# S5 tables moved behind the SSD stage in wider operations, the convolution's tail queued one block later, and the first loads interleaved

## The chip, the cores and the metric

One core of one Trainium2 chip runs the program. Engines: TensorE (PE; its weight loads, PEld, overlap the products), VectorE (DVE), ScalarE (ACT), GpSimd (POOL) and SyncE (SP, which only issues transfers here). ACT, POOL and SP each have a queue of DMA issues that stand in order between the engine's other instructions. The metric is the device time of one execution in microseconds (us); less is better.

## The reference

A decoder step with two layers on 576 tokens: a prompt of 512 and eight sequences of 8 new tokens. Each layer's token mixer runs three branches on the same input and merges them with gates:

```python
gates, u, q, k, v, fg, z, xbc, dt_raw = split(h @ w_in[l])
y_s5, s5_re, s5_im = s5_branch(u, ...)
y_fox = fox_prompt(q, k, v, logf)
xbc_c = silu(causal_conv(xbc))
y_ssd, h_new = ssd_scan(...)
merged = gates0*(y_s5 @ w_s5) + gates1*(y_fox @ w_fox) + gates2*(y_ssd @ w_ssd)
out = merged @ w_o[l]
```

The S5 branch is a complex diagonal state space in 32 groups of 16 channels and 64 states: `x[t] = A x[t-1] + B u[t]`, `y = Re(C x) + D u`, with A and B made from `lam`, `log_dt` and `b` by a discretisation. The SSD branch takes a causal convolution of width 4 over 1024 channels, `silu`, and a scan in chunks of 128. After the mixer come a layer norm and a channel mixer: a dense SwiGLU in layer 0, eight experts in layer 1.

## The kernel before, in words

**Products.** An activation is kept as two tiles, `xh` and `xl` (a rounded part and its rest), and so is each weight block. `colblocks` (L297) goes over blocks of 128 columns of a weight: `wload` (L252) puts a load of 512 KB on SP's queue (three buffers `wr`), `wsplit` (L270) splits it in halves with a copy on ScalarE (`wh`, L98) and a subtraction on VectorE (`wl`, L107), and `mm3` (L285) makes 24 products a half-block of 288 tokens (L291 to L293) into one of two accumulators `mm`. A whole block is 48 products; "block" below means one of these.

**Head.** `load_x` (L235) loads five tiles of x (four of 128 prompt tokens, one of 64 sample tokens), transposes each in eight pieces on TensorE (L233) and splits the result. Then `u_proj` projects the S5 input `u` in half-blocks, four of the first 288 tokens and four of the rest. Hooks behind half-blocks call `load_params` (small parameter loads `prow` and `tokp`, a transposition, a few VectorE operations; `dexp`, L127, is an exponential by polynomial on VectorE, with tiles `ef` and `eki`) and `s5_prep(0)`.

**S5 tables.** `s5_prep` (L332) discretises, builds powers of A (`pw`, nine of them) and then, for four quarters of the groups, the tables `ca` (C times powers 0 to 8) and `bm` (B times powers 0 to 7). It goes power by power, with operations of 4 groups x 16 channels = 64 columns; `ca` on VectorE, `bm` on GpSimd in layer 0 and on VectorE in layer 1. The temporaries lie in `s5a`. `bm` is transposed to `bo`, a short convolution kernel is formed by products with `bbd` (L466) into `kz`, and the three tables go to DRAM (`CD`, `BD`, `KZ`) over GpSimd's queue. In layer 1 the tables are made inside the feed-forward stage before it.

**Convolution.** `conv` (L1001) projects the 1024 convolution channels, eight blocks. `ev_x` takes each accumulator out of PSUM: ScalarE copies it to `xp` (L98), and behind the second half the taps run for 512 prompt columns and 64 sample columns: one scaled copy on ScalarE into `cva` (L1024), three fused multiply-adds each on VectorE (L110); then a Tanh on ScalarE into `cvt` (L1027), one more VectorE operation, and a store to `XD` on ScalarE's queue (L1029). `xp`, `cva`, `cvt` share a ring of four buffers.

**The rest of the mixer.** `ssd` (chunks: masks `ma`, `mt`, loads `xc` of `XD`, products `yd`), `kqv_fox` (12 blocks of keys, queries and values, with prompt attention per head: `pf`, `pT`, `vt`, `kT`, `qT`), `s5_scan_and_out` (L479: state inputs from `UD` and `BD` as `bmu`, a scan on VectorE, then four groups of output products with `tu`, `cu` and `V`, L587 and L588, a Gelu, a store and a reload), `fox_sample` (pairs of sequences: paged keys `kpg` and values `vpg`, scores `pa` L949, outputs `po` L986), fillers (gate and z blocks), `s5_glu` (a gated linear unit on `y5h`) and `merge5`.

**Order.** The code is written stage by stage, but a scheduler sets each engine's order from the dependencies and a priority that follows the order in the code. So stages overlap: before the convolution ends the next stage's work stands between its products, and moving a call moves its instructions on every engine.

Of the kernel before, what the change touches and what calls it, by code (L numbers as in the profile page):

```python
# [19 lines left out]
P = 128  # L20
# [26 lines left out]
def decoder_step(ctx, tc, A, O):  # L47
# [187 lines left out]
    def load_x():  # L235
        xs = A["x_sample"].rearrange("b t d -> (b t) d")
        for i in range(5):
            n = P if i < 4 else 64
            src = A["x_prompt"][0, i * P:(i + 1) * P, :] if i < 4 else xs
            xt = U("A", [P, D], name="xt")  # L240
            sp.dma_start(out=xt[:n], in_=src)
            for k0 in (0, 4):
                pt = (PX, PF)[k0 // 4]("xp")
                pv = pt.rearrange("p (k t) -> p k t", k=4)
                for k in range(4):
                    tr(pv[:, k, :n], xt[:n, (k0 + k) * P:(k0 + k + 1) * P], n)
                s = slice(i * P, i * P + n)
                split(xh[:, k0:k0 + 4, s], xl[:, k0:k0 + 4, s], pv[:, :, :n])
# [83 lines left out]
    def s5_prep(l):  # L332
# [23 lines left out]
        t256 = s5a[:, 672:928].rearrange("p (g c) -> p g c", g=16)  # L356
# [79 lines left out]
        for q in range(4):  # L436
# [4 lines left out]
            t_, t2_ = t256[:, 0:4], t256[:, 4:8]  # L441
            cr, ci = cc[:, 0, gs], cc[:, 1, gs]
            for tau in range(9):
                pr_, pi_ = bc(pw[:, 0, tau, gs], 2, 16), bc(pw[:, 1, tau, gs], 2, 16)
                o0, o1 = ca[:, 0, :, tau, :], ca[:, 1, :, tau, :]
                mul(en, o0, cr, pr_)
                mul(en, t_, ci, pi_)
                sub(en, o0, o0, t_)
                mul(en, o1, cr, pi_)
                mul(en, t_, ci, pr_)  # L450
                stt(o1, o1, -1.0, t_, OP.mult, OP.subtract)
            for s in range(8):
                pr_, pi_ = bc(pw[:, 0, s, gs], 2, 16), bc(pw[:, 1, s, gs], 2, 16)
                cmul(dve if l else pool, bm[:, 0, :, s, :], bm[:, 1, :, s, :], pr_, pi_, bb[:, 0, gs], bb[:, 1, gs], t2_)
# [213 lines left out]
    def u_proj(l, hooks=()):  # L668
        us = {}

        def ev_u(j, h, o):
# [9 lines left out]
            for at, f in hooks:  # L681
                if (j, h) == at:
                    f(0)
# [1248 lines left out]
```

## Time and profile before

| what | value |
|---|---|
| median of 3 runs | 2440.81 us (2440.51 to 2442.37) |
| the profiled execution, its own time | 2439.51 us |
| its span in the profile | 2437.9 us |
| mean granted clock of TensorE | 0.966 |
| PE busy | 2282.9 us (94%) |
| PEld busy | 2158.8 us (89%) |
| DVE busy | 1621.9 us (67%) |
| ACT busy | 1144.4 us (47%) |
| POOL busy | 596.0 us (24%) |

The span runs from the first to the last instruction of the profiled execution; 1.6 us lie around it. "Busy" is the time in which an engine works, and its share of the span. The granted clock is 1 at full speed. A table of stretches gives busy time for pieces of the span; a wait is put down to what ended last before the waiting instruction started. The list by line groups like instructions; in it a line such as L101 or L107 can be that of a helper (`mul`, `sub`), so the tile names tell what it is.

### The profile page before, as it was taken

How to read it: one execution, taken by the hardware profiler on the slowest of the kernel's cores; microseconds unless marked ns; L12 is line 12 of the kernel's file. 1: busy time of each engine (PE TensorE's matmuls, PEld its weight loads, DVE VectorE, ACT ScalarE, POOL GpSimd, SP SyncE). 2: the span in 40 equal slices, each digit the busy share in tenths (PEclk: the TensorE clock that was granted, in tenths of full speed). 3: DMA queues.
4: the chain of work that ended last, by engine and by line, in shares of the span. 5: the costliest groups of instructions: out<-in, count | busy, mean ns of one | idle time of the engine just before them, and what ended most of it. 6: DMA issues, size and time to landing. Idle time of an engine off the chain costs nothing. (4 is left out here: it accounts for less than half of the span.)

```text
span 2437.9 us, 46161 instructions
## 1 busy us (share of the span) xinstructions
PE 2282.9 (94%) x17037; PEld 2158.8 (89%) x17038; DVE 1621.9 (67%) x4287; ACT 1144.4 (47%) x2553; POOL 596.0 (24%) x879
## 2 busy tenths in 40 slices
PE   8889998889999999999999999898999699999975
PEld 7889887679998999999899888788999599999974
DVE  7986695446478883334765975555447588888856
ACT  4435434425346323223654443353334477777753
POOL 5874233441020110000214332244003410000022
PEclk9999998889999999999999999999999799999997
DMA  8367558473345433223575575766333799999993
GB/s 203 108 209 202 171 158 203 120 228 94 93 134 133 117 121 105 81 87 94 135 207 166 152 184 156 169 182 204 88 92 113 209 267 255 255 256 253 254 256 86
DMA packets 591997, 402.32 MB, mean 165 GB/s; under 512 B 59254, under 2 KB 556199, under 8 KB 591731
## 3 DMA queue, kind: packets, MB, share of 16 engines
q1 hardware_dynamic: 480088, 240.75, 37.3%
q0 software_dynamic: 29008, 90.07, 13.4%
q10 hardware_dynamic: 82666, 68.46, 9.7%
q8 instruction: 136, 2.23, 0.4%
q14 instruction: 99, 0.80, 0.1%
HBM read 330.74 MB, written 68.57 MB: 164 GB/s over the span
## 5 line engine op out<-in xcount | busy, mean ns | idle before, releaser
L107 DVE TENSOR_TENSOR wl<-wr,wh 128x512 fp32r<-128x512 f32 x894 | 622.7, 707 | 382.4 <-ACT wh L98 359.3
L98 ACT ACTIVATE wh<-wr 128x512 fp32r<-128x512 f32 x894 | 552.6, 625 | 523.6 <-PE mm L292 366.7
L291 PE MATMUL mm<-xh,wh 128*128 128x288 f32 (+1 forms) x2048 | 618.9, 302 | 21.3 <-ACT xp L98 10.3
L292 PE MATMUL mm<-xl,wh 128*128 128x288 f32 (+1 forms) x2048 | 614.8, 300 | 0.0
L293 PE MATMUL mm<-xh,wl 128*128 128x288 f32 (+1 forms) x2048 | 612.1, 299 | 0.0
L291 PEld LDWEIGHTS mm<-xh,wh 128*128 128x128 f32 (+1 forms) x2048 | 387.4, 189 | 34.6 <-ACT xp L98 11.5
L292 PEld LDWEIGHTS mm<-xl,wh 128*128 128x128 f32 (+1 forms) x2048 | 387.5, 189 | 6.7 <-issue 4.4
L293 PEld LDWEIGHTS mm<-xh,wl 128*128 128x128 f32 (+1 forms) x2048 | 387.1, 189 | 3.6 <-issue 1.1
L1674 PE MATMUL mm<-xe,wh 128*128 128x352 f32 x448 | 132.1, 356 | 0.0
L1674 PE MATMUL pf<-xe,wh 128*128 128x352 f32 x448 | 130.5, 355 | 0.0
L1675 PE MATMUL pf<-xe,wl 128*128 128x176 f32 x512 | 117.3, 249 | 0.0
L1675 PE MATMUL mm<-xe,wl 128*128 128x176 f32 x512 | 117.1, 249 | 0.0
L291 PE MATMUL mm<-hq,wh 128*128 128x288 f32 x352 | 104.5, 297 | 0.2 <-DVE rf L104 0.2
L293 PE MATMUL mm<-hq,wl 128*128 128x288 f32 x352 | 104.2, 296 | 0.0
L292 PE MATMUL pf<-xl,wh 128*128 128x288 f32 x352 | 104.1, 296 | 0.0
L291 PE MATMUL pf<-xh,wh 128*128 128x288 f32 x352 | 103.9, 295 | 0.0
L293 PE MATMUL pf<-xh,wl 128*128 128x288 f32 x352 | 103.9, 295 | 0.0
L292 PE MATMUL mm<-hq,wh 128*128 128x288 f32 x352 | 103.7, 295 | 0.0
L1675 PEld LDWEIGHTS mm<-xe,wl 128*128 128x128 f32 x512 | 96.6, 192 | 0.0
L1675 PEld LDWEIGHTS pf<-xe,wl 128*128 128x128 f32 x512 | 96.6, 192 | 0.0
L110 DVE SCALAR_TENSOR_TENSOR gt<-gt,mm 128x288 f32<-128x288 f32 x96 | 43.3, 452 | 67.5 <-PE mm L293 52.9
L1674 PEld LDWEIGHTS mm<-xe,wh 128*128 128x128 f32 x448 | 85.4, 191 | 0.0
(665 smaller groups left out, 5448.2 us busy)
## 6 DMA issues: line engine op xcount, KB each, us to landing
wr<-in_w_in_dram SPq DMA_DIRECT2D x112, 512.0 KB
wr<-in_moe_w_gate_dram SPq DMA_DIRECT2D x64, 512.0 KB
wr<-in_moe_w_up_dram SPq DMA_DIRECT2D x64, 512.0 KB
wr<-in_moe_w_down_dram SPq DMA_DIRECT2D x64, 512.0 KB
wr<-in_w_o_dram SPq DMA_DIRECT2D x32, 512.0 KB
wr<-in_ffn_w_gate_dram SPq DMA_DIRECT2D x25, 512.0 KB
wr<-in_ffn_w_up_dram SPq DMA_DIRECT2D x25, 512.0 KB
wr<-in_ffn_w_down_dram SPq DMA_DIRECT2D x24, 448.0 KB
```

What stands on the lines that cost most here:

```text
L98: return act.activation(out, in_, AF.Copy)
L107: e.tensor_tensor(out, a, b, op=OP.subtract)
L110: dve.scalar_tensor_tensor(out, a, s, b, op0=op0, op1=op1)
L291: pe.matmul(o, lhsT=wh_[:, a, :m], rhs=x[0][:, k, s], start=(st and k == 0), stop=False)
L292: pe.matmul(o, lhsT=wh_[:, a, :m], rhs=x[1][:, k, s], start=False, stop=False)
L293: pe.matmul(o, lhsT=wl_[:, a, :m], rhs=x[0][:, k, s], start=False, stop=(sp_ and k == kt - 1))
L1674: pe.matmul(o, lhsT=h_[:, k % 4, :], rhs=xf, start=(k == 0), stop=False)
L1675: pe.matmul(o[:, 0:CAP], lhsT=l_[:, k % 4, :], rhs=x[:, k, 0], start=False, stop=False, skip_group_check=True)
```

## The change

Three parts of the mixer's start and one temporary:

- **Head.** `load_x` is cut into `x_dma` and `x_tr`. SP's queue gets three x tiles, the weights of the first two half-blocks (loaded ahead and handed to `colblocks` as `first`), then the other two x tiles; the transpositions of x tiles 3 and 4 become hooks behind the first and second half-block, the parameter loads a hook behind the third, the parameters' transposition one behind the first half-block of the second 288 tokens.
- **Convolution tail.** The Tanh, the last VectorE operation and the store of a block are kept as `pend` and issued with the next block, ordered behind the copy that empties its second accumulator. The result overwrites the input tile `xp`; `cvt` is gone. The two small GpSimd copies to `co` come first.
- **Tables.** `s5_prep(0)` is called behind `ssd(0)` in the code, not as a hook of the `u` projection. In both layers `ca` is made for all nine powers in one operation (576 columns) and `bm` for all eight (512 columns), six operations each per quarter. A new temporary `s5t` holds the intermediate products. `bm` stays on GpSimd in layer 0.

```diff
-    def load_x():
...
+    def x_dma(i):
...
+        sp.dma_start(out=xt[:n], in_=src)
+
+    def x_tr(i):
...
-    def colblocks(src, c0, ncol, kt, x, evac, by_half=False):
+    def colblocks(src, c0, ncol, kt, x, evac, by_half=False, first=()):
+        first = list(first)
...
-                w = wsplit(wload(src, c0 + j * P, P, kt), P, kt)
+                w = wsplit(first.pop(0) if first else wload(src, c0 + j * P, P, kt), P, kt)
...
+        s5t = U("R" if l else "A", [P, 1152], name="s5t")
...
-            t_, t2_ = t256[:, 0:4], t256[:, 4:8]
-            cr, ci = cc[:, 0, gs], cc[:, 1, gs]
-            for tau in range(9):
-                pr_, pi_ = bc(pw[:, 0, tau, gs], 2, 16), bc(pw[:, 1, tau, gs], 2, 16)
-                o0, o1 = ca[:, 0, :, tau, :], ca[:, 1, :, tau, :]
-                mul(en, o0, cr, pr_)
...
-            for s in range(8):
...
-                cmul(dve if l else pool, bm[:, 0, :, s, :], bm[:, 1, :, s, :], pr_, pi_, bb[:, 0, gs], bb[:, 1, gs], t2_)
+            t_ = s5t[:, 0:576].rearrange("p (g t c) -> p g t c", g=4, t=9)
+            t2_ = s5t[:, 576:1088].rearrange("p (g t c) -> p g t c", g=4, t=8)
+            cr, ci = bc(cc[:, 0, gs], 2, 9), bc(cc[:, 1, gs], 2, 9)
+            pr_, pi_ = [bc(pw[:, i, :, gs].rearrange("p t g -> p g t"), 3, 16) for i in range(2)]
+            o0, o1 = ca[:, 0], ca[:, 1]
+            mul(en, o0, cr, pr_)
+            mul(en, t_, ci, pi_)
+            sub(en, o0, o0, t_)
+            mul(en, o1, cr, pi_)
+            mul(en, t_, ci, pr_)
+            stt(o1, o1, -1.0, t_, OP.mult, OP.subtract)
+            cmul(dve if l else pool, bm[:, 0], bm[:, 1], pr_[:, :, 0:8], pi_[:, :, 0:8],
+                 bc(bb[:, 0, gs], 2, 8), bc(bb[:, 1, gs], 2, 8), t2_)
...
         conv(l, w_in)
         ssd(l)
+        if l == 0:
+            s5_prep(0)
         kqv_fox(l, w_in)
...
+        def tail(j, x, a_, after):
+            t_ = x[:, 0:T]
+            with tc.issue_after(after.ins) if after is not None else nullcontext():
+                act.activation(t_, a_, AF.Tanh)
+                stt(t_, t_, 1.0, a_, OP.add, OP.mult)
+                act.dma_start(out=XD[l][j], in_=t_)
+        pend = []
...
+            i_ = cp(xs_[:, :, 3:11], o[:, 224:288].rearrange("p (b t) -> p b t", b=8))
...
+            if pend:
+                tail(*pend.pop(), i_)
...
-            act.activation(t_, a_, AF.Tanh)
-            stt(t_, t_, 1.0, a_, OP.add, OP.mult)
-            act.dma_start(out=XD[l][j], in_=t_)
...
+            pend.append((j, x, a_))
         colblocks(w_in, C_XBC, 1024, 8, X, ev_x)
+        tail(*pend.pop(), None)
...
-        load_x()
-        u_proj(0, (((1,0), load_params), ((0,1), s5_prep)))
+        for i in range(3):
+            x_dma(i)
+        uw = [wload(A["w_in"][0], C_U + j * P, P, 8) for j in range(2)]
+        for i in (3, 4):
+            x_dma(i)
+        for i in range(3):
+            x_tr(i)
+        u_proj(0, (((0, 0), lambda: x_tr(3)), ((1, 0), lambda: x_tr(4)), ((2, 0), lambda: params_dma(0)),
+                   ((0, 1), lambda: params_tr(0))), uw)
         mixer(0)
```

In the rows of order below, a row is one instruction (or several alike, x4) with its line, the tile it writes, the tiles it reads and the shape. A load of `wr` is a weight block's.

SyncE's queue at the head, before and then now:

```order
L221 DMA lb<-in_page_table_dram 128x16
L241 DMA xt<-in_x_prompt_dram 128x1024 x4
L241 DMA xt<-in_x_sample_dram 64x1024
L262 DMA wr<-in_w_in_dram 128x8x128 x2
L653 DMA prow<-in_b_gate_dram 24x128
```

```order
L221 DMA lb<-in_page_table_dram 128x16
L241 DMA xt<-in_x_prompt_dram 128x1024 x3
L266 DMA wr<-in_w_in_dram 128x8x128 x2
L241 DMA xt<-in_x_prompt_dram 128x1024
L241 DMA xt<-in_x_sample_dram 64x1024
L266 DMA wr<-in_w_in_dram 128x8x128
L664 DMA prow<-in_b_gate_dram 24x128
```

Two weight loads moved ahead of the last x tiles, and the parameter loads (`prow` and on, 13 in all) behind a third. The 14 table loads, which stood behind six `wr` loads, now stand behind all eight of the `u` projection and the eight of the convolution.

VectorE in the stretch around one convolution block, before and then now (`ssp` belongs to the forget gate's logarithm):

```order
L101 TENSOR_TENSOR s5a<-s5b,s5a 128x64
L101 TENSOR_TENSOR ssp<-ssp 128x80
L107 TENSOR_TENSOR wl<-wr,wh 128x512
L110 SCALAR_TENSOR_TENSOR cva<-xp,prm_184,cva 128x512
L110 SCALAR_TENSOR_TENSOR cva<-xp,prm_184,cva 128x64
L107 TENSOR_TENSOR ca<-ca,s5a 128x4x16
L720 TENSOR_SCALAR ssp<-ssp 128x80
L107 TENSOR_TENSOR wl<-wr,wh 128x512
L110 SCALAR_TENSOR_TENSOR kz<-id_78,dq,p_776 128x16
L1009 MEMSET xp 128x3
L1013 COPY xp<-cs_1421 128x8x3
```

```order
L110 SCALAR_TENSOR_TENSOR xp<-xp,cva 128x576
L734 TENSOR_SCALAR ssp<-ssp 128x80
L110 SCALAR_TENSOR_TENSOR cva<-xp,prm_184,cva 128x512
L1033 MEMSET xp 128x3
L1037 COPY xp<-cs_728 128x8x3
L101 TENSOR_TENSOR ssp<-ssp 128x80
L110 SCALAR_TENSOR_TENSOR cva<-xp,prm_184,cva 128x64
L110 SCALAR_TENSOR_TENSOR cva<-xp,prm_184,cva 128x512
L734 TENSOR_SCALAR ssp<-ssp 128x80
L110 SCALAR_TENSOR_TENSOR cva<-xp,prm_184,cva 128x64
L110 SCALAR_TENSOR_TENSOR cva<-xp,prm_184,cva 128x512
```

The 64-column operations on `s5a`, `ca` and the `kz` are gone from between the block's taps, and the operation that finishes a block (`xp<-xp,cva`, before on `cvt`) stands among the next block's.

TensorE where the first S5 output product with the state (`V`) comes; `mm` rows are a filler block's last products. Before and then now:

```order
L291 MATMUL mm<-xh,wh 128x288
L292 MATMUL mm<-xl,wh 128x288
L293 MATMUL mm<-xh,wl 128x288
L861 MATMUL pf<-pT,vt 64x128 x2
L588 MATMUL p_4679<-V_4344,cu 128x72
L587 MATMUL p_4679<-uc_4326,tu 128x72
```

```order
L297 MATMUL mm<-xh,wl 128x288
L233 MATMUL px<-ident,kpg 128x128
L877 MATMUL pf<-pT,vt 64x128 x2
L233 MATMUL pf<-ident,s 128x128 x3
L854 MATMUL pf<-kT,qT 128x384 x2
L965 MATMUL pa<-kk,lq 32x256 x2
L877 MATMUL pf<-pT,vt 64x128 x3
L854 MATMUL pf<-kT,qT 128x512 x2
L877 MATMUL pf<-pT,vt 64x128 x4
L593 MATMUL p_4312<-V_3977,cu 128x72
L592 MATMUL p_4312<-uc_3959,tu 128x72
```

The output products moved behind attention scores (`kT,qT`), sample scores (`kk,lq`) and page transpositions (`kpg`), and behind the last of the filler blocks: before, one of the 36 blocks ahead of the S5 output stood behind the first of them. Earlier in TensorE's order, the last product with `bbd` stands behind 21 blocks before and 24 now. The first product of the gated unit (`y5h`) stood behind the first of the four sample pairs (`po`) before and stands behind the second now.

## Rows read from the trace of the kernel before

**Rows 1.** stretches: us; PE, PEld, DVE, ACT, POOL busy (instructions); clock, DMA, GB/s

```profile
60.00:160.00 100.00, 82.88 (x601) 79.25 (x600) 99.11 (x324) 43.57 (x96) 88.22 (x198) 0.94 0.49 149
160.00:300.00 140.00, 139.98 (x1105) 129.44 (x1105) 91.68 (x228) 65.45 (x165) 52.55 (x82) 0.98 0.69 192
850.00:900.00 50.00, 50.00 (x402) 49.28 (x402) 42.74 (x203) 14.95 (x27) 8.56 (x10) 1.00 0.43 130
```

**Rows 2.** waits of TensorE, 60 to 160 us: engine, line, releaser: us, times, longest

```profile
PE mm L291 <- ACT xp L98: 9.4, 4, 3.8
PE yd L1109 <- DVE mt L101: 5.3, 1, 5.3
```

**Rows 3.** VectorE's groups, 0 to 300 us: count, busy us, mean ns, idle before

```profile
L101 DVE TENSOR_TENSOR s5a<-s5b,s5a 128x64 f32<-128x64 f32 x72 | 21.3, 296 | 0.8
L101 DVE TENSOR_TENSOR ca<-s5b,s5a 128x64 f32<-128x64 f32 x72 | 19.0, 326 | 0.0
L107 DVE TENSOR_TENSOR ca<-ca,s5a 128x64 f32<-128x64 f32 x36 | 12.3, 342 | 0.5
L110 DVE SCALAR_TENSOR_TENSOR ca<-ca,s5a 128x64 f32<-128x64 f32 x36 | 10.1, 280 | 0.4
L101 DVE TENSOR_TENSOR ma<-tri,ads 128x512 fp32r<-128x512 f32 x8 | 7.9, 990 | 0.0
L101 DVE TENSOR_TENSOR mt<-mt,bt 128x512 f32<-128x512 f32 x8 | 5.5, 702 | 0.2
```

**Rows 4.** GpSimd's groups, 0 to 300 us, the same columns

```profile
L101 POOL TENSOR_TENSOR s5a<-s5a,s5b 128x64 f32<-128x64 f32 x64 | 26.3, 410 | 3.8
L104 POOL TENSOR_TENSOR bm<-bm,s5a 128x64 f32<-128x64 f32 x32 | 19.7, 616 | 2.1
L101 POOL TENSOR_TENSOR bm<-s5a,s5b 128x64 f32<-128x64 f32 x64 | 18.2, 319 | 0.1
L101 POOL TENSOR_TENSOR ma<-tri,ads 128x512 fp32r<-128x512 f32 x8 | 9.4, 1179 | 0.0
```

**Rows 5.** TensorE in order of time, head: start, us, work [idle before <- releaser]

```profile
5.89 5.35 PE L233 MATMUL xp<-ident,xt 128*128 128x128 f32 x24 [5.89 <-DMA xt<-in_x_prompt_dram]
15.69 0.61 PE L291 MATMUL mm<-xh,wh 128*128 128x288 f32 x1 [1.64 <-ACT wh L98]
19.41 0.41 PE L233 MATMUL px<-ident,prow 104*128 104x104 f32 x1 [2.88 <-DMA tokp<-in_b_fgate_dram]
```

**Rows 6.** accumulators emptied, layers 0 and 1: min/median/max ns, first to last start

```profile
L98 ACT ACTIVATE xp<-mm x24: 218/348/415, 59.3 to 129.6; 128x288 f32<-128x288 f32 x8, 128x224 f32<-128x224 f32 x8, 128x64 f32<-128x64 f32 x8
L98 ACT ACTIVATE xp<-mm x24: 219/340/412, 1241.6 to 1295.1; 128x288 f32<-128x288 f32 x8, 128x224 f32<-128x224 f32 x8, 128x64 f32<-128x64 f32 x8
```

**Rows 7.** who waited for the convolution's VectorE chain, layer 0: us, times

```profile
  ACT cvt L1027: 14.6, 6
```

**Rows 8.** the S5 chain's places in order of time, TensorE and ScalarE's queue

```profile
211.82 0.67 PE L466 MATMUL p<-ca,bbd 128*32 128x128 f32 x16
241.48 0.27 PE L233 MATMUL p<-ident,sh 128*128 128x128 f32 x1
242.08 0.33 ACTq L497 DMA_DIRECT2D bmu<-BD  x1
386.12 0.44 PE L588 MATMUL p<-V,cu 128*128 128x72 f32 x2
406.01 0.41 PE L838 MATMUL pf<-kT,qT 128*128 128x128 f32 x2 [2.40 <-DMA qT<-QD]
451.00 0.85 PE L291 MATMUL mm<-y5h,wh 128*128 128x288 f32 x2 [0.16 <-ACT y5h L117]
460.81 1.07 PE L949 MATMUL pa<-kk,lq 128*32 128x256 f32 x4
467.50 0.62 PE L986 MATMUL po<-vpg,pTs 128*32 128x128 f32 x16
```

**Rows 9.** a table product of layer 1 on VectorE, 560 to 960 us

```profile
L101 DVE TENSOR_TENSOR s5a<-s5b,s5a 128x64 f32<-128x64 f32 x72 | 16.0, 222 | 0.1
```

More of the change, by code (lines that the diff above doesn't have):

```diff
@@ L233, in tr @@
         pe.transpose(out, in_, ident[:n, :n])
-    def load_x():
[L236 to L248, printed above, removed]
+    xts = {}
+    def x_dma(i):
+        n = P if i < 4 else 64
+        src = A["x_prompt"][0, i * P:(i + 1) * P, :] if i < 4 else A["x_sample"].rearrange("b t d -> (b t) d")
+        xts[i] = xt = U("A", [P, D], name="xt")
+        sp.dma_start(out=xt[:n], in_=src)
+    def x_tr(i):
+        n = P if i < 4 else 64
+        xt = xts[i]
+        for k0 in (0, 4):
+            pt = (PX, PF)[k0 // 4]("xp")
+            pv = pt.rearrange("p (k t) -> p k t", k=4)
+            for k in range(4):
+                tr(pv[:, k, :n], xt[:n, (k0 + k) * P:(k0 + k + 1) * P], n)
+            s = slice(i * P, i * P + n)
+            split(xh[:, k0:k0 + 4, s], xl[:, k0:k0 + 4, s], pv[:, :, :n])
     WB = dict(pool=wp, wr=3, wh=4, wl=4, body=False)
@@ L353, in s5_prep @@
         s5b = UA([P, 1152], name="s5b")
+        s5t = U("R" if l else "A", [P, 1152], name="s5t")
         sm = s5a[:, 0:384].rearrange("p (a g) -> p a g", g=16)
         pw = s5a[:, 384:672].rearrange("p (i t g) -> p i t g", i=2, t=9)
-        t256 = s5a[:, 672:928].rearrange("p (g c) -> p g c", g=16)
+        t256 = s5t[:, 0:256].rearrange("p (g c) -> p g c", g=16)
         bb = s5b[:, 0:512].rearrange("p (i g c) -> p i g c", i=2, g=16)
@@ L643, in decoder_step, with params_dma @@
     R_BG, R_L1G, R_L1B, R_L2G, R_L2B, R_CW, R_CB, R_GLU, R_NW = 0, 24, 32, 40, 48, 56, 88, 96, 100
+    prow = {}
     def load_params(l):
-        rows = V5("prow")[:104, 0:P]
+        params_dma(l)
+        params_tr(l)
+    def params_dma(l):
+        prow[l] = rows = V5("prow")[:104, 0:P]
         for nm, r0, n in (("b_gate", R_BG, 24), ("ln1_g", R_L1G, 8), ("ln1_b", R_L1B, 8), ("ln2_g", R_L2G, 8),
@@ L653, in load_params, with params_tr @@
             sp.dma_start(out=rows[r0:r0 + n], in_=s.rearrange("(r c) -> r c", c=P))
+        for i, nm in enumerate(("b_fgate", "ssd_dt_bias", "ssd_a_log", "ssd_d")):
+            sp.dma_start(out=tokp[l][:, i * 8:(i + 1) * 8], in_=A[nm][l].unsqueeze(0).to_broadcast([P, 8]))
+    def params_tr(l):
+        rows = prow[l]
         pt = PX()
@@ L660, in load_params @@
         dve.tensor_scalar(bglu[l], prm[l][:, R_GLU:R_GLU + 4], 0.5, None, op0=OP.mult)
-        for i, nm in enumerate(("b_fgate", "ssd_dt_bias", "ssd_a_log", "ssd_d")):
-            sp.dma_start(out=tokp[l][:, i * 8:(i + 1) * 8], in_=A[nm][l].unsqueeze(0).to_broadcast([P, 8]))
         dexp(tokp[l][:, 16:24], tokp[l][:, 16:24], 8)
@@ L666, in decoder_step, with u_proj @@
     S = dict(nc=nc)
-    def u_proj(l, hooks=()):
+    def u_proj(l, hooks=(), first=()):
         us = {}
@@ L682, in ev_u @@
                 if (j, h) == at:
-                    f(0)
-        colblocks(A["w_in"][l], C_U, 512, 8, X, ev_u, by_half=True)
+                    f()
+        colblocks(A["w_in"][l], C_U, 512, 8, X, ev_u, by_half=True, first=first)
     def mixer(l):
@@ L1016, in ev_x @@
             cp(x[:, 291:515], o[:, 0:224])
-            cp(xs_[:, :, 3:11], o[:, 224:288].rearrange("p (b t) -> p b t", b=8))
+            i_ = cp(xs_[:, :, 3:11], o[:, 224:288].rearrange("p (b t) -> p b t", b=8))
+            pool.tensor_copy(co[:, j, 0:3], x[:, 512:515])
+            pool.tensor_copy(co[:, j, 3:27].rearrange("p (b t) -> p b t", b=8), xs_[:, :, 8:11])
+            if pend:
+                tail(*pend.pop(), i_)
             wc = lambda q: pr[:, R_CW + q * 8 + j:R_CW + q * 8 + j + 1]
@@ L1020, in ev_x @@
             a_ = wk.tile([P, T], F32, name="cva", tag="xp", bufs=4)
-            t_ = wk.tile([P, T], F32, name="cvt", tag="xp", bufs=4)
             for dst, src in ((a_[:, 0:512], lambda q: x[:, q:q + 512]),
```

8 lines of the change are left out of this document (removed).

## Prediction

> **What bounds the kernel now.** I read the summary of busy time first (the table above): TensorE works 94% of the span, so only stretches in which it waits, or works at the lower clock, can give time back. The table of stretches shows such a place near the start [rows 1]: from 60 to 160 us TensorE is busy 82.88 of 100 us and its granted clock is 0.94, while VectorE is busy 99.11 of 100 and GpSimd 88.22. From 160 to 300 us the picture is turned round: TensorE 139.98 of 140, VectorE 91.68. The waits name what TensorE lacked [rows 2]: 9.4 us for ScalarE to empty a convolution block's accumulator (four waits) and 5.3 us for a VectorE product of the SSD stage. That is 14.7 of the 17.1 us missing between 60 and 160. The list by line and shape says what fills VectorE there [rows 3]: 216 operations of 64 columns on `ca`, 21.3 + 19.0 + 12.3 + 10.1 = 62.7 us; and GpSimd [rows 4]: 160 of 192 on `bm`, 26.3 + 19.7 + 18.2 = 64.2 us (32 subtractions come to these). These are the first layer's S5 tables. **VectorE, loaded with tables, paces the convolution.** After it TensorE is the bound, with VectorE a third idle.
>
> **The change part by part.**
>
> *Head.* Before, the first product starts at 15.69 us [rows 5], behind five loads of x, and the second group waits another 2.88 us for the parameters' transposition, which stands second in TensorE's order. The first x tile is used at 5.89; between there and 15.69 some 1.75 MB of x and 0.5 MB of weights arrive in 9.8 us, 0.23 MB/us. In the new order 0.75 MB (x tile 4 and the samples) stand behind the first weights: 0.75/0.23 = 3.3 us earlier. The 2.88 us go too. Against that, the 16 held-back transpositions now fall between products, the second half-block's first product stands in the first one's sequence and waits for the second weights, and VectorE's `ef` reads the parameter load before it splits the third half-block. I take 3.5 us; the ends are 0 and 6.2.
>
> *Convolution.* What do eight blocks cost without tables beside them? The same loop runs in layer 1, where no tables are made. From the first to the last emptying of an accumulator there are 129.6 - 59.3 = 70.3 us in layer 0 and 1295.1 - 1241.6 = 53.5 us in layer 1 [rows 6]: **17 us**. The queued tail belongs to this term: ScalarE now waits 14.6 us in six places for VectorE's chain before its Tanh [rows 7], with the next block's weight split and emptying queued behind. Behind the next block's emptying that wait is covered by the block's 48 products, 6.0 us at 402 TensorE instructions in 50 us [rows 1]. Its own price without the tables is about nothing: layer 1 has the Tanh wait too and keeps the pace of its products. Using the input tile for the result frees one of the ring's four slots; I count nothing for it. Some small VectorE work of the discretisation stays in the stage, so 17 is taken with ends 10 and 17.
>
> *SSD stage.* The wait of 5.3 us [rows 2] comes from a VectorE that is still behind; the 2.4 us that these two waits leave of the 17.1 I take for shorter ones of the same kind. Of both together 7.5 us go; if the moved tables hold VectorE there, nothing goes.
>
> *Tables.* They don't vanish: 24 operations of 576 columns replace 216. The nearest row without GpSimd beside it is 702 ns for 512 columns, the nearest with it 990 ns [rows 3]: 0.79 or 1.11 us each, 19 or 27 us in place of 62.7. On GpSimd 24 operations of 512 columns at 1.179 us [rows 4] make 28 us in place of more than 64. They land in the stretch that has 48 us of VectorE to spare [rows 1] and which loses the old tables' second half, so they cost nothing on the path; without that cover it would be up to 27 us. TensorE's part (16 products in 0.67 us [rows 8] and eight transpositions a group) only changes place: the two groups that ran inside the convolution come back later, 3 us by that row.
>
> That the chip's port weighs long GpSimd operations differently is a rule to set against this. The row: a 64-column product takes 296 ns beside GpSimd's tables [rows 3] and 222 ns in layer 1 without them [rows 9], so it is stretched by a third, not held for the 410 ns of a GpSimd product [rows 4]. The Trainium skill ("SBUF — State Buffer", section "SBUF: two separate sides") says the shared port pair is an exclusive lock, and that the loser blocks for the whole instruction; by that rule longer GpSimd operations would hold VectorE longer, and the trace agrees only in part. By the row the sum below stands; by the rule it would come out as rival 3 does.
>
> *Queues.* The tables' 14 loads leave SP's place ahead of the convolution's weights and now stand ahead of the attention weights, covered by three weight buffers. Their 12 stores move on GpSimd's queue to a place among the loads of `xc`, keys and queries, and those loads stand there behind the long operations too: six a group, 6 x 1.179 us [rows 4] = 7 us at most for one load. I count nothing, since TensorE has projections to do beside the attention, and 7 us as the upper end.
>
> *Layer 1.* Its tables are made in the feed-forward stage, where such products were 72 of 222 ns [rows 9] and become 8: less work for VectorE, but TensorE is busy 50.00 of 50 beside it [rows 1]. Nothing.
>
> Up to the 24th of the 36 weight blocks that are done before the S5 output this makes -3.5 - 17 - 7.5 + 3 = **-25 us**.
>
> **What of it reaches the end.** The S5 branch is a chain: tables, state inputs, scan, four output groups, store and reload, gated linear unit, merge. Its last table product stands behind block 21 before and block 24 now. Before, block 24 passes at 241.48 us [rows 8]; less 25 that is 216.5, against 211.82. So the chain starts 5 us later than it did, while all else is 25 us early. It has slack: the tables were in memory soon after 212, yet the first group's state inputs were asked for only at 242.08 [rows 8], by ScalarE's order. In the new order the first S5 output product with the state stands behind all filler blocks, which end at about 406.01; less 25 that is 381, against 386.12: 5 us gained there. From there to the gated unit's start at 451.00 [rows 8] were 64.9 us for four groups with attention heads between; one head and a half stood there, now half a head, so I take 4 us off. Behind the gated unit's start stood one pair of the sample attention (from 460.81 to 467.50, 7 us), which the new order has ahead of it. 5 + 4 + 7 = 16, if the chain decides; 25 if TensorE's work does. I take **18**: nearer the chain, since it has the tighter rows.
>
> The profiled execution took 2439.5 us; less 18 that is 2421.5. The median of the runs is 1.3 above it, so I forecast **2422.5**, with 2412 to 2431 as its own range.
>
> **Rivals.** (1) *All of it arrives and more.* If the output groups, freed of the filler, follow each other without pause, the 25 and the 7 add: 2440.8 - 32 = 2409. For it: TensorE waits in the stretch behind 406, as for the 2.40 us there [rows 8]. Chance 0.12. (2) *The chain keeps its length.* Table to gated unit took 451.0 - 211.8 = 239 us; starting 5 us later and saving only the 7 behind it, the end moves by 2: 2439. Against it: the slack to 242.08. Chance 0.10. (3) *GpSimd's long operations hold VectorE.* If each of 24 blocks VectorE for its 1.179 us, 28 us are added to 27 of tables in a stretch with 48 to spare; VectorE would again pace TensorE and a loss like that of the old stage, 17 us, comes back: 2440. Against it the third by which rows are stretched. Chance 0.05. (4) *Slower: the S5 chain decides and the convolution gains little.* If ScalarE or the loads hold the convolution back so that only 10 us are gained up to block 24, the last table product comes at 231.5, 20 us late; with the chain's old length, less 7, the end is 13 us late: 2454. It decides from a table product later than 219 (211.8 + 7). Against it: layer 1's pace. Chance 0.07.
>
> **Numbers.** Forecast 0.66, rivals 0.12, 0.10, 0.05, 0.07. A difference under 0.2%, 4.9 us, can't be told from none. Faster: forecast, rival 1, and the edge of rivals 2 and 3, 0.80; same 0.13; slower 0.07. The range from 2404 to 2439 leaves out rival 4 and the far end of rival 1.
>
> **What would show it.** Right: the spacing of the first and last accumulator emptying in layer 0 falls from 70 to some 55 us; the 60 to 160 stretch has TensorE near 98 of 100 at clock 1.0; `ca` has 24 rows of 0.8 to 1.1 us; the first product is at 12 to 13 us; the gated unit starts at 435 to 445. Wrong: VectorE still above 95% in the convolution; a wait of TensorE on an S5 product after block 25; the gated unit at or behind 451; or a stall of the attention weights behind the table loads.

## The result: slower by 0.74%

| | median | range | runs |
|---|---|---|---|
| before | 2440.35 us | 2436.07 to 2446.29 | 8 |
| changed | 2456.69 us | 2449.07 to 2468.85 | 8 |

The ratio is 1.0074, with a 95% interval of 1.0056 to 1.0092. On another chip, timed again beside the kernel before, it was 1.0093 (1.0060 to 1.0126). The forecast was a gain of 0.75%, with a chance of 0.07 for slower; the time lies outside its range.

The profiled execution of the changed kernel is its longest run, 2468.85 us (span 2467.2), 12 us over the median. In it the first products and the emptied accumulators of the convolution answer to [rows 5] and [rows 6]; TensorE's timeline first, then the accumulators of layer 0 and layer 1:

```profile
12.34 0.40 PE L295 MATMUL mm<-xh,wh 128*128 128x288 f32 x1 [1.26 <-ACT wh L98]
```

```profile
L98 ACT ACTIVATE xp<-mm x24: 220/340/415, 55.0 to 105.4; 128x288 f32<-128x288 f32 x8, 128x224 f32<-128x224 f32 x8, 128x64 f32<-128x64 f32 x8
L98 ACT ACTIVATE xp<-mm x24: 220/340/414, 1260.8 to 1312.6; 128x288 f32<-128x288 f32 x8, 128x224 f32<-128x224 f32 x8, 128x64 f32<-128x64 f32 x8
```

So the head is 3.35 us earlier and the convolution takes 50.4 us from first to last emptying, where it took 70.3. What came behind it is seen in the table of stretches, its columns as in [rows 1]:

```profile
60.00:160.00 100.00, 88.50 (x649) 86.73 (x649) 84.27 (x252) 49.27 (x105) 40.37 (x60) 0.93 0.52 150
160.00:300.00 140.00, 126.87 (x979) 113.72 (x978) 103.86 (x174) 58.73 (x153) 63.61 (x72) 0.96 0.65 192
850.00:900.00 50.00, 50.00 (x412) 48.91 (x411) 31.24 (x57) 16.24 (x32) 7.01 (x11) 1.00 0.43 139
```

TensorE now lacks 13.1 us in a stretch (160 to 300 us) in which it had lacked 0.02, and VectorE is busy 103.86 us there in place of 91.68, with fewer instructions (174 in place of 228). TensorE's waits from 60 to 300 us, columns as in [rows 2]:

```profile
PE yd L1133 <- DVE mt L101: 14.2, 2, 10.0
PE p L233 <- DVE smx L861: 3.0, 1, 3.0
PE pf L854 <- DVE s L110: 2.4, 1, 2.4
```

The accumulators' waits (9.4 us) are gone; the SSD products' wait for VectorE's `mt` has grown from 5.3 to 14.2 us. The longest, 9.97 us, ends at 140.05 us, and what follows it runs at half the clock for 6.5 us (the table of stretches again):

```profile
130.00:140.00 10.00, 0.07 (x1) 0.00 (x0) 10.00 (x16) 0.69 (x2) 6.78 (x8) 0.65 0.45 148
140.00:146.50 6.50, 6.45 (x28) 6.45 (x29) 2.90 (x14) 0.60 (x1) 0.00 (x0) 0.50 0.60 189
146.50:152.00 5.50, 5.50 (x43) 5.50 (x42) 1.36 (x3) 2.35 (x5) 2.26 (x3) 0.99 0.29 86
```

The operations that took the place of those in [rows 3] and [rows 4], VectorE and then GpSimd, 0 to 300 us:

```profile
L101 DVE TENSOR_TENSOR ca<-s5b,s5a 128x576 f32<-128x576 f32 x8 | 8.8, 1135 | 0.0
L107 DVE TENSOR_TENSOR ca<-ca,s5t 128x576 f32<-128x576 f32 x4 | 8.3, 2077 | 0.0
L101 DVE TENSOR_TENSOR s5t<-s5b,s5a 128x576 f32<-128x576 f32 x8 | 8.0, 1001 | 0.0
L799 DVE COPY qS<-kq 128x64 f32<-128x64 f32 x4 | 3.6, 891 | 2.8 <-ACT kq L798 2.8
L110 DVE SCALAR_TENSOR_TENSOR ca<-ca,s5t 128x576 f32<-128x576 f32 x4 | 3.4, 839 | 0.0
L101 DVE TENSOR_TENSOR ptmp<-s5a 128x32 f32<-128x32 f32 x2 | 2.7, 1346 | 0.0
```

```profile
L101 POOL TENSOR_TENSOR bm<-s5a,s5b 128x512 f32<-128x512 f32 x8 | 10.4, 1312 | 3.2 <-PE p L233 3.1
L101 POOL TENSOR_TENSOR s5t<-s5a,s5b 128x512 f32<-128x512 f32 x8 | 9.4, 1179 | 0.2
L104 POOL TENSOR_TENSOR bm<-bm,s5t 128x512 f32<-128x512 f32 x4 | 5.6, 1400 | 0.0
L107 POOL TENSOR_TENSOR bm<-bm,s5t 128x512 f32<-128x512 f32 x4 | 5.5, 1378 | 0.0
```

The tables' own time is near the prediction's upper estimate: 28.5 us on VectorE (27 there) and 30.9 on GpSimd (28). But these means hide two kinds of operation. Of the two products of 32 columns (mean 1346 ns) one took 0.18 us and one 2.51; of the four `ca` subtractions (mean 2077 ns) two took 0.74, one 1.60 and one 5.22. Time order shows what the long ones stood for. VectorE, then GpSimd (start, us, work):

```profile
127.65 1.14 DVE L419 COPY a<-s5a 128x32 f32<-128x32 f32 x1
...
130.96 1.28 DVE L101 TENSOR_TENSOR a<-a 128x16 f32<-128x16 f32 x1
132.16 0.16 DVE L101 TENSOR_TENSOR ptmp<-a 128x16 f32<-128x16 f32 x1
132.25 0.16 DVE L101 TENSOR_TENSOR a<-a 128x16 f32<-128x16 f32 x1
...
211.56 5.22 DVE L107 TENSOR_TENSOR ca<-ca,s5t 128x576 f32<-128x576 f32 x1
```

```profile
126.11 2.64 POOL L101 TENSOR_TENSOR bm<-s5a,s5b 128x512 f32<-128x512 f32 x2
...
130.93 1.27 POOL L107 TENSOR_TENSOR kq<-kq,kqh 128x512 fp32r<-128x512 f32 x1
132.13 0.55 POOL L846 DMA_DIRECT2D qT<-QD  x1
...
211.91 1.12 POOL L101 TENSOR_TENSOR s5t<-s5a,s5b 128x512 f32<-128x512 f32 x1
212.99 1.04 POOL L101 TENSOR_TENSOR ma<-tri,ads 128x512 fp32r<-128x512 f32 x1
213.99 2.17 POOL L101 TENSOR_TENSOR bm<-s5a,s5b 128x512 f32<-128x512 f32 x2
```

The 16-column product that starts 0.03 us behind GpSimd's `kq` ends 0.04 us behind its end, after 1.28 us; the next ones, with only a transfer's issue beside them, take 0.16. The copy from 127.65 ends at 128.79, when the pair of `bm` products does (128.75). **VectorE is held until GpSimd's operation ends**, and the subtraction from 211.56 was held through four of them in a row: it ends at 216.78, 0.62 us behind the last.

To put a number on it, for each single VectorE instruction in the timeline I take its duration less the median of the same operation and shape with no GpSimd instruction beside it, and add up what is over 0.15 us ("held time" below). From 100 to 250 us it is 13.1 us before and 34.3 in the changed kernel. In the 10 us in which TensorE waits for `mt` VectorE is busy without a pause, and about 5 of them are held time; the rest is the work itself, of the tables and the stage.

Last, the S5 chain, to set beside [rows 8]:

```profile
241.97 0.67 PE L471 MATMUL p<-ca,bbd 128*32 128x128 f32 x16
412.50 0.44 PE L593 MATMUL p<-V,cu 128*128 128x72 f32 x2
475.64 0.38 PE L295 MATMUL mm<-y5h,wh 128*128 128x288 f32 x1
```

Every step is late: the last table product by 30.2 us, the first output product by 26.4, the gated unit by 24.6. The first product with `yfh`, behind the mixer, is 11.8 us late. Between the last table product and the first output product the lateness shrinks and then grows: the state inputs are asked for 15.5 us late, the scan on VectorE ends 25.7 late (390.6 against 364.9), and a copy of `V` that GpSimd issues behind the scan comes 33.6 late. GpSimd before, then now:

```profile
371.71 0.54 POOL L569 DMA_DIRECT2D V<-V  x1
```

```profile
400.69 1.16 POOL L573 COPY vx<-V 64x1168 f32<-64x1168 f32 x1 [8.43 <-DVE wl L107]
405.30 0.56 POOL L574 DMA_DIRECT2D V<-V  x1
```

Two cautions for reading single profiles. The kernel before was profiled again on a chip where it runs slower (2464.01 us). There the first product came at 24.41 us in place of 15.69 and `yfh` at 564.38 in place of 543.76, so that a later stretch can differ by 20 us between two profiles of one kernel. The 9.99 us of idle time ahead of that first product are put down to nothing that the profile shows (`issue`):

```profile
24.41 0.61 PE L291 MATMUL mm<-xh,wh 128*128 128x288 f32 x1 [9.99 <-issue]
564.38 0.29 PE L291 MATMUL mm<-yfh,wh 128*128 128x288 f32 x1
```

I therefore read ratios (each against the kernel before on the same chip) for the end, and profiles for what happens up to some 300 us, where two profiles of one kernel differ by what the head gave and little else. The second caution is layer 1's mixer. From its first `px<-sq,br` product to its first with `yfh` it took 496.3 us in place of 482.2, on the other chip 492.5 in place of 484.1.

### The profile page after: what moved, and what is told of

Same layout as the page of the kernel before. It is cut to its first block, busy times and chain, and to the rows that moved or that the text cites. A ratio compares the mean times of both kernels' runs of the same rounds, so it can differ in the third digit from the quotient of the medians.

```text
span 2467.2 us, 45473 instructions
## 1 busy us (share of the span) xinstructions
PE 2299.8 (93%) x17037; PEld 2170.4 (88%) x17038; DVE 1581.3 (64%) x3735; ACT 1147.2 (46%) x2555; POOL 549.5 (22%) x711
```

## The experiments

Theory A: GpSimd's 512-column operations hold VectorE. Theory B: the tables stand ahead of what TensorE waits for, the hold is small. Theories C and D came later and stand with their runs. Experiments e1 to e4 ran on one chip, e5, e6 and the two repeats (c1, c2) on one, e7 to e10 on one, e11 to e14 on one, e15 and e16 on one.

**c1, c2: both kernels again.** No edit.

> The kernel before, once more, for a profile on the same chip as the next three runs: in the first study of experiments all four kernels had 7 to 9 us more in the first two blocks and 10 to 12 us more in the expert stage than both first profiles. If that belongs to the chip, the same shows here; if it belongs to the kernels, this profile is like the first one.

> The changed kernel once more, timed beside the next two. Theory A and B: a ratio of 1.005 to 1.010, its block 24 near that of the kernel before.

c1: 2464.01 us, with the late first product above. Its second block passes 4.9 us later than in the first profile of before, c2's 7.5 us later than in the first profile of the changed kernel, so the late first blocks of e1 to e4 are not of those kernels' making. (Blocks are counted by their own products, 48 each, without the transpositions that share the accumulators.) The longer expert stage doesn't show alike: from layer 1's `yfh` to the end c1 takes 763.7 us and c2 764.1, the first profiles 759.7 and 763.2, e1 to e4 761 to 771. c2: 1.0093. The changed kernel's lead over c1 is 22.8 us at the 16th block and gone at the 24th (0.2 us behind), its last table product is 29.9 us later. So the first profile's picture up to 250 us repeats.

**e1: `bm` on VectorE.**

```diff
-            cmul(dve if l else pool, bm[:, 0], bm[:, 1], pr_[:, :, 0:8], pi_[:, :, 0:8],
+            cmul(dve, bm[:, 0], bm[:, 1], pr_[:, :, 0:8], pi_[:, :, 0:8],
```

> The changed kernel, with the 24 bm operations of layer 0 on VectorE instead of GpSimd (as layer 1 has them). Theory A (GpSimd's 512-column operations hold VectorE until they end, and this is what loses the 24 us between the 16th and the 24th weight block): although VectorE gets 24 x 0.7 = 17 us more to do, its short operations lose their 1.0 to 1.3 us durations; block 24 passes before 235 us (241.3 in the changed kernel), time 2440 to 2448, at least 8 us under the changed kernel's 2456.7. Theory B (the tables stand in VectorE's order ahead of what TensorE waits for in the SSD stage, the holding is small): VectorE has 17 us more ahead of the same products, time 2457 to 2470.

Ratio 0.9959 (0.9941 to 0.9978), 2430 us on the first chip's scale, even below A's range: this one line turns a loss of 0.74 to 0.93% into a gain of 0.4%. Held time from 100 to 250 us is 15.3 us. Theory B's 2457 to 2470 us would be no better than the changed kernel's ratio, so B falls as the main cause. The wait for `mt`, 14.2 us in the changed kernel, is nearly gone:

```profile
PE yd L1133 <- DVE mt L101: 0.7, 1, 0.7
```

The last table product comes at 211.7 us, as before. Block 24 passed at 239.3 us, outside A's 235, in a profile whose second block already passes 8.8 us later than the changed kernel's (39.9 against 31.1).

**e2: the tables at the old place, in wide operations.**

```diff
-        if l == 0:
-            s5_prep(0)
...
-                   ((0, 1), lambda: params_tr(0))), uw)
+                   ((0, 1), lambda: (params_tr(0), s5_prep(0)))), uw)
```

> The changed kernel with s5_prep(0) called where it was before (a hook in the u projection), in the wide operations. Theory B: the convolution has VectorE at about 90% instead of 99%, the 16th block passes at 135 to 140 us (153.4 before, 129.6 changed), the SSD stage keeps its pace, and the chain of the S5 branch starts at 150 to 180 us; time 2420 to 2430, faster than both kernels. Theory A: GpSimd's long operations hold VectorE inside the convolution, which stays as slow as before (16th block at 145 to 155 us): 2435 to 2445.

0.9994 (0.9973 to 1.0015): no gain. The emptying of the accumulators takes 80.8 us, longer than the 70.3 before:

```profile
L98 ACT ACTIVATE xp<-mm x24: 219/350/413, 65.1 to 145.9; 128x288 f32<-128x288 f32 x8, 128x224 f32<-128x224 f32 x8, 128x64 f32<-128x64 f32 x8
```

VectorE's held time from 50 to 100 us goes from 0.7 to 10.3 us. The time is in A's range (2439 us on the first chip's scale), the 16th block, at 168 us, is later than either theory had it. Theory B's gain isn't there; fewer and longer operations are no gain beside the convolution while half of them are GpSimd's.

**e3: moved, but with the old 64-column operations.** The loops over powers put back in place of the six wide operations.

> The changed kernel with the old 64-column operations for the tables in both layers, still called behind the SSD stage. Theory B: VectorE has 36 us more in the SSD stage than with wide operations, the last table product comes at 260 us or later (242.0 changed, 211.8 before), time 2470 to 2485. Theory A: the single holds are shorter (0.3 to 0.6 us), so that SSD products wait less, though the tables end later: 2450 to 2465.

1.0175 (1.0146 to 1.0203), 2483 us on the first chip's scale: in B's range and far over A's. Held time is 9.8 us, as A says, but the last table product comes at 330.2 us, where B had only "260 us or later". The holds are not all that counts: the time goes with the tables' end here, which A had not priced.

**e4: head and tail alone; e14: the head alone.** The tables at the old place in the old operations; in e14 the convolution's tail as before too.

> Only the head's interleaving and the queued convolution tail of the change: the tables at the old place in the old 64-column operations. Both theories: the head gives its 3.3 us, the tail gives a part of the 9.4 us of waits for an emptied accumulator, and nothing is lost later in layer 0: 2428 to 2437. If the tail costs time in layer 1 (there the changed kernel lost 14 us from 1204 to 1704), this shows here as well: 2440 to 2450.

> The kernel before with the head's interleaving alone. By the prediction's term of 3.5 us and the chain that takes it up: ratio 0.998 to 1.000. If the head gives nothing to the end: 0.999 to 1.001; the first product comes 3 to 12 us earlier either way.

1.0002 (0.9981 to 1.0023) and 1.0019 (1.0002 to 1.0036). e4's first expectation is missed; its time lies in the second range, but not for its reason, since layer 1's mixer takes 480.6 us there, less than before. e14's lies over both of its ranges, though its interval reaches into them. The first product comes at 11.7 and 11.8 us, but VectorE still paces the convolution; e14 is 5.0 us early at the second block and 4.6 late at the tenth. The head gives nothing at the end by itself.

e4 shows one thing more. Beside c1, whose first blocks are as late, its last table product comes 21 us later (239.4 against 218.4), its state inputs 8.5 and its first output product 6.1; for c2 these are 30, 14.1 and 31.3 us. So tables 21 us late cost nothing at the end there.

**e5, e6: idle work on GpSimd.** e1, with operations added at the place that `bm` had, into columns that nobody reads: 24 products, or 52 writes of zeros.

```diff
+            i0_ = mul(en, o0, cr, pr_)
+            if l == 0:
+                dm_ = s5a[:, 672:1152]
+                with tc.issue_after(i0_.ins):
+                    for k_ in range(6):
+                        mul(pool, dm_, s5b[:, 0:480], s5b[:, 0:480])
```

> e1_bm_vector (bm on VectorE) with 24 products added on GpSimd, 480 columns, two inputs in SBUF, at the place where bm stood in the changed kernel; nobody reads their result. Theory A (a GpSimd operation that reads SBUF holds VectorE until it ends): VectorE's operations between 100 and 250 us are stretched by 30 us or more over what they take alone (34.4 in the changed kernel, 15.3 in e1), and the time goes from e1's ratio 0.996 to 1.003 or more. Theory B (bm was late, or stood in a chain): nothing waits for these products, so 0.994 to 0.998.

> The same with 52 writes of zeros of 480 columns (about 0.5 us each) in place of the 24 products, so that GpSimd and its queue of transfers are held up as long, but it reads nothing from SBUF. If what costs is GpSimd's queue (transfers of xc, keys and queries issued late), the time is that of e5 (1.003 or more). Theory A: VectorE isn't stretched, ratio 0.994 to 0.999.

(The diff is e5's; e6 has 13 calls of `memset` a quarter in place of the six products.) e5: 1.0025 (1.0001 to 1.0049), held time 31.4 us. e6: 0.9959 (0.9939 to 0.9979), held time 16.7, near e1's 15.3. VectorE's weight splits and GpSimd's added work, 100 to 250 us, in e5 and then in e6:

```profile
L107 DVE TENSOR_TENSOR wl<-wr,wh 128x512 fp32r<-128x512 f32 x28 | 25.2, 899 | 2.4 <-ACT wh L98 1.5 <-PE p L233 0.6
L101 POOL TENSOR_TENSOR s5a<-s5b 128x480 f32<-128x480 f32 x24 | 29.4, 1225 | 0.6
```

```profile
L107 DVE TENSOR_TENSOR wl<-wr,wh 128x512 fp32r<-128x512 f32 x29 | 19.8, 684 | 6.5 <-ACT wh L98 6.0
L457 POOL MEMSET s5a<- 128x480 f32 x52 | 26.9, 517 | 1.4
```

In e5 five of the weight splits took 1.1 to 3.3 us and the rest 0.67 to 0.69; in e6 none took more than 0.69. The same span of GpSimd time, 29.4 and 26.9 us, costs 0.66% (16 us) when it reads SBUF and nothing when it only writes. Transfers that GpSimd issues late behind its operations, alike in both, are not the cause. **The hold is shown, at 16 us**, on a kernel whose VectorE makes `bm` as well; that it costs as much in the changed kernel, with nearly the same held time, is taken over and not measured. That the Trainium skill ("SBUF — State Buffer", section "SBUF: two separate sides") gives an exclusive lock, taken against a two-input VectorE operation only by a GpSimd operation that reads SBUF, agrees with both runs.

**e12: the tables late, without GpSimd.** 1.0093 - 1.0025 leaves 0.7% of the changed kernel's loss that e5 doesn't have. Theory D: it is the S5 chain.

```diff
         ssd(l)
+        kqv_fox(l, w_in)
         if l == 0:
             s5_prep(0)
-        kqv_fox(l, w_in)
```

(on e1)

> e1_bm_vector with the tables called behind the keys, queries and attention in the code: no GpSimd operation of the tables, but the last table product comes at 250 us or later (248 in the changed kernel, 212 in e1). Theory D (half of the changed kernel's loss is the S5 chain, which starts 30 us late): ratio 1.002 to 1.010, the gated unit starts at 475 us or later. If the hold alone costs: 0.994 to 0.998.

1.0142 (1.0123 to 1.0161), over D's range. VectorE is held no more than before (11.6 us) and TensorE is far ahead: block 28 passes 33.2 us earlier than in the first profile of before, with 145.24 of 150 us busy from 100 to 250. But:

```profile
298.76 0.67 PE L471 MATMUL p<-ca,bbd 128*32 128x128 f32 x16 [0.30 <-ACT bo L98]
511.81 0.85 PE L295 MATMUL mm<-y5h,wh 128*128 128x288 f32 x2 [11.23 <-ACT y5h L117]
```

The gated unit waits for the S5 branch and starts 60.8 us later than in that profile. From 400 to 550 us:

```profile
400.00:550.00 150.00, 92.02 (x698) 76.27 (x698) 60.96 (x216) 36.76 (x82) 48.05 (x65) 0.70 0.42 105
```

TensorE is busy 92.02 of 150 us, and its clock is down to 0.70. **The chain that begins with the tables ends layer 0's mixer here**; TensorE's lead up to the 28th block is worth nothing if the tables come this late, 57 us behind the changed kernel's. The price is not the tables' lateness alone: TensorE also waits 28.6 us for the pages of keys (`kpg`; 7.0 before), and the copy of `V` comes at 452.7 us, 27.6 us behind the scan's end (6.8 before), with GpSimd's loads of pages ahead of it in its queue.

**e13: the tables early, on GpSimd.** The changed kernel with `s5_prep(0)` between `conv` and `ssd`.

> The changed kernel (bm on GpSimd) with the tables between the convolution and the SSD stage. Theory D: the last table product comes at 220 us or earlier, the hold of VectorE stays (30 us of stretched operations between 100 and 250 us): ratio 1.001 to 1.004, as e5, in place of 1.009. If only the hold costs: 1.007 or more.

1.0054 (1.0034 to 1.0074), between the two. Its condition did not come about: the last table product stays at 241.0 us, though the tables are called earlier, with 35.3 us held. That these 30 us come of making `bm` on GpSimd (e1 has 211.7 at the changed kernel's place) is what this adds; how much of the 0.7% is the chain's it doesn't settle. The trace of the changed kernel shows a part of how: between its first and last `bm` operation (126 to 235 us) GpSimd is busy 64.83 of 109 us, and its longest wait is for a transfer that stands ahead of the next `bm` operation in its queue:

```profile
POOL vt L838 <- DMA VD<-tok: 8.7, 1, 8.7
```

Another 21 us go on waits for VectorE ahead of the stores of earlier quarters (`CD`, `KZ`). e6 could not show this, since nobody waits for its zeros.

**e7, e8: the convolution's tail.** On e1: the tail queued in layer 0 alone, or nowhere.

```diff
-            pend.append((j, x, a_))
+            if l:
+                tail(j, x, a_, None)
+            else:
+                pend.append((j, x, a_))
```

> e1_bm_vector with the queued convolution tail in layer 0 alone; in layer 1 each block's Tanh, last operation and store are issued at once, as before. Theory C (the queued tail costs layer 1 some 8 us: in the changed kernel layer 1's mixer loses 9 to 14 us, and in e1 it gives back 12 of the 19 us that it was ahead): ratio 0.991 to 0.993. Rival: what layer 1 loses comes from elsewhere or from one profile's chance, ratio 0.995 to 0.997 as e1.

> e1_bm_vector without the queued tail in either layer. If the tables' leaving is what speeds the convolution up (17 of 17 us in the prediction, the tail nothing), block 16 passes within 3 us of e1's 137.9 and the ratio is that of e7. If the tail is a part of it, block 16 passes 5 us later or more and the ratio is 0.003 above e7's.

0.9938 (0.9919 to 0.9957) and 0.9948 (0.9924 to 0.9972); e7's lies between its two forecasts, and both intervals reach e1's. e8's accumulators take 51.4 us without any queued tail, and its 16th block passes 0.3 us behind e1's (138.7 and 138.4 us): it is the tables' leaving that frees the convolution, not the tail. Theory C has the profiles against it: in the nine kernels' profiles whose layer 1 is the changed kernel's (changed, c2, e1, e2, e5, e6, e10, e12, e13) its mixer takes 475 to 496 us, in the eight without a queued tail there (before, c1, e7, e8, e11, e14 to e16) 482 to 489. The same code spreads by 21 us, and the tail makes no difference that shows.

**e9: less on GpSimd.** On e1, the `kq` and `kql` subtractions and `xdd` on VectorE in both layers.

> e1_bm_vector with two more kinds of 512-column GpSimd operations on VectorE: the subtractions for keys and queries (kq, kql) and the product xdd, in both layers. Theory A: 12 operations of 1.1 to 1.4 us no longer hold VectorE in the stretch of layer 0 that paces, VectorE gets 12 x 0.7 = 8 us more; its stretched time between 100 and 250 us falls from 15 to 5 us, ratio 0.992 to 0.995. Theory B (VectorE's load decides): 0.998 to 1.000.

0.9982 (0.9961 to 1.0003), in B's range and a miss for A, though held time fell to 7.4 us and TensorE was 17.6 us ahead of c1 at block 28, where e1 was 8.8. Layer 1's mixer, 493.0 us in this profile where c1 has 484.1, gives 9 us back, which is within the spread just named. That the holds left in e1 cost time is not shown by it.

**e10, e11, e16, e15: towards a better kernel.** e10 is e1 with the tables called between the convolution and the SSD stage. e11 adds e7's tail; e16 is e11 again; e15 is e11 with e9's operations on VectorE in layer 0 alone.

```diff
         conv(l, w_in)
-        ssd(l)
         if l == 0:
             s5_prep(0)
+        ssd(l)
         kqv_fox(l, w_in)
```

> e1_bm_vector with the tables called between the convolution and the SSD stage, so that they stand ahead of it in each engine's order. If the S5 chain (last table product at 211.7 us in e1, as before, while TensorE is 20 us early) holds the end of the mixer, the last table product comes at 185 to 195 us, the gated unit starts 10 us earlier and the ratio is 0.991 to 0.994. If TensorE's own waits decide, the SSD products wait for VectorE behind the tables, and the ratio is 0.996 to 1.000.

> e10 (bm on VectorE, tables between convolution and SSD stage) with the queued tail in layer 0 alone, as in e7. If the two gains add (0.003 and 0.002 against e1): ratio 0.990 to 0.992, faster than both kernels. If they are one and the same or chance: 0.992 to 0.996.

> e11 once more on the same chip as e15, for the comparison: 0.990 to 0.994.

> e11 with the key and query subtractions and the product xdd of layer 0 alone on VectorE (e9 had them there in both layers: TensorE was 22 us early at block 28, and layer 1 gave 9 us back). If the holds that are left in layer 0 (11.6 us between 100 and 250 us) still cost: ratio 0.987 to 0.990, beside 0.992 of e11. If the S5 chain or a chance of one profile decided in e9: 0.990 to 0.995.

e10: 0.9927 (0.9903 to 0.9952). e11: 0.9917 (0.9900 to 0.9934), median 2423.38 us; again as e16, 0.9924 (0.9901 to 0.9946). e15: 0.9902 (0.9886 to 0.9918). All beat the kernel before, and by their ratios the changed kernel; the intervals of e11 and e15 reach into both of their forecasts. e15's interval overlaps those of e11 and e16, so that the holds which are left still cost is likely, not shown. In e11 the chain is early at both ends:

```profile
200.02 0.67 PE L471 MATMUL p<-ca,bbd 128*32 128x128 f32 x16 [0.20 <-ACT bo L98]
445.27 0.38 PE L295 MATMUL mm<-y5h,wh 128*128 128x288 f32 x1
```

e10, e11 and e16 had their last table product at 209.9, 200.0 and 207.9 us, not at the 185 to 195 that e10 was expected to have, and e10's gated unit starts at 458.3 us, not earlier than e1's (450.6). e10's time came as forecast, but not by those signs; what gave it is not shown.

## Why the prediction was wrong, step by step

- **What bounds the kernel.** Right: VectorE, loaded with tables, paced the convolution. Without them it takes 50.4 us, and 51.4 without the tail too.
- **Head, 3.5 us.** Right at its place (3.35, and 4.3 by the fourth block), but worth nothing alone (e14). Between c1 and c2 the first product gains 12.3 us and the second block only 1.4.
- **Convolution, 17 us; the tail, nothing.** Right, somewhat small: TensorE is 23.8 us ahead at the 16th block, head included, where the two terms make 20.5.
- **SSD stage, "Of both together 7.5 us go".** Wrong in sign: the wait for `mt` went from 5.3 to 14.2 us. The sentence went on "if the moved tables hold VectorE there, nothing goes", with no end below nothing.
- **Tables, "cost nothing on the path" and "3 us by that row".** The failed step. The working compared busy time with VectorE's 48 spare us and stretched the wide operations by the row of 990 ns. The tables' own time came out near that (28.5 us, 27 by the row). But what is held is not only the tables: the stage's other operations are held as well when they meet a GpSimd operation, a 16-column product for 1.28 us in place of 0.16. Held time went from 13.1 to 34.3 us, and the lead was gone at the 24th block. e1, with `bm` on VectorE, takes the loss away, and e5 and e6 put the hold at 0.66%.
- **The port: "stretched by a third, not held for the 410 ns".** This is where it was lost. 296 against 222 ns is a mean over 72 products, and their median before was 225 (count; min/median/max ns):

```profile
L101 DVE TENSOR_TENSOR s5a<-s5b,s5a x72: 206/225/1578, 54.9 to 175.1; 128x64 f32<-128x64 f32 x72
```

Of the 72, 44 took 206 to 227 ns, as without GpSimd, and 28 took 293 or more, up to 1578; a mean of the two looks like a stretch. The trace of before had it. The rule that the prediction set against its row agrees with e5 and e6. Rival 3, built on it, had a chance of 0.05; its mechanism came true, but its price, 28 us that only give the gain back (2440 us), was too low by 17 us, since it held the tables alone and left the S5 chain out.
- **Queues, nothing, at most 7 us.** The term asked what long operations do to the loads behind them. It left out the other way round: `bm` stands behind GpSimd's transfers and their waits (8.7 us once), a part of why the tables end 30 us late.
- **Sum at the 24th block, -25 us.** Measured 0.4 us behind in the first profile (241.6 against 241.2), 0.2 behind between c2 and c1: the lead of 23.8 at the 16th block is used up within eight blocks. Even with `bm` on VectorE only 8.1 us of it are left there (e1 against c1).
- **"The chain starts 5 us later".** 30.2 us later. The slack that I saw, from 211.82 to 242.08, took half of that: the state inputs were asked for at 257.54 us, 15.5 late. Behind them the chain lost time again, to the scan's end and the copy of `V`, and the first output product came 26.4 late; between c1 and c2 the same places are 14.1, 29.1, 35.7 and 31.3 late. Why the copy waits is open: the two profiles name different releasers.
- **Rival 4.** It set the point at a table product later than 219 us and the time at 2454; measured were 242 and 2456.7. That the times agree is luck: by its own sum, lateness less 7 us, 242 would give 2464, and e4 lost nothing with its tables 21 us late. Its cause was wrong as well: the convolution gained all that it could, and the tables were late because of where and on which engine they were made. Its chance, 0.07, came from asking only whether the convolution would fail.
- **Layer 1, nothing.** Its tables stage cost nothing, as forecast (TensorE is 11.8 us late where that stage begins and 11.7 where it ends). Its mixer was 8 to 14 us longer in two profiles; since one and the same code took 475 to 496 us in nine, this is not shown to be the change's.

The 1.15 to 1.34% between the changed kernel and e1 come of one line, `bm` on GpSimd. A hold of that size is shown to cost 0.66%. The rest stays open. It goes with a last table product 24 us later than e5's (248.3 against 224.2, same chip), and e12 shows that tables later still cost time. Against the tables' lateness as the whole of it stands e4, which lost nothing with tables 21 us late (c2: 30), and e13 did not separate the two; what the chain loses behind its state inputs was not varied.

## What to carry to other kernels

Before work is made into fewer, longer operations on GpSimd, look at VectorE's shortest operations in time order beside it: if they end when GpSimd's do, the length of GpSimd's operation is the price for each that meets it early, several in a row can be the price for one, and a mean duration hides this. Where a stretch is freed by moving work behind it, ask which chain starts with the moved work and when its last piece comes; a lead on the busiest engine is worth nothing if that chain ends the stage.

## What the runs showed of the hardware that was not expected

- GpSimd products of 480 columns with their inputs in SBUF (1225 ns each) raised VectorE's weight splits from 684 to 899 ns on average (e5): five of 28 took 1.1 to 3.3 us. Writes of zeros over the same columns (517 ns each) left them at 684 (e6).
- An operation of VectorE with 16 columns took 1.28 us beside GpSimd's `kq` and 0.16 us right behind it; one of 576 columns took 5.22 us beside four GpSimd operations in a row, two others of its kind 0.74. A sum with one input in PSUM (`yt<-yd,yt`, 512 columns) took its usual 0.68 us from 160.35, beside two `bm` products.
- Behind a wait of 9.97 us TensorE's granted clock was 0.50 from 140.0 to 146.5 us (28 products) and 0.99 in the 5.5 us behind that (43 products).
- The same kernel, profiled on two chips, had its first product at 15.69 and at 24.41 us, and medians of one kernel over chips went from 2440 to 2465 us, so that only ratios on one chip could be compared.
